# A two-layer attention backbone on one core: the row of maxima by one matmul and a copy, the modulation bias added at eviction, the last tiles' outputs in another order

## The chip, the core and the metric

The kernel runs on one core of a Trainium2 chip. Five engines work side by side, each through its own list of instructions in order: TensorE (PE, matmuls; PEld are its weight loads), VectorE (DVE), ScalarE (ACT), GpSimd (POOL) and SyncE (SP), which here issues nearly all DMAs. An engine whose next instruction waits holds up everything behind it in its list. Matmul results lie in PSUM banks and must be read out by DVE or ACT before a bank can be used again. The metric is the device time of one execution in microseconds, the median of three runs.

## The reference

Two layers over 1024 latent tokens and 256 context tokens of width 1024. Both layers modulate their input and gate their output by a vector made from the conditioning, `silu(c) @ w_mod + b_mod`; the first mixes by grouped-query attention, the second by neighbourhood attention, which leaves the context as it is.

```python
for i in range(DEPTH):
    mod_x = (silu_c @ w_mod[i] + b_mod[i])[:, None, :]
    mod_c = silu_cc @ w_mod[i] + b_mod[i]
    sh_x, sc_x, g_x = jnp.split(mod_x, 3, axis=-1)      # and sh_c, sc_c, g_c
    hx = rms_norm(x, norm_g[i]) * (1.0 + sc_x) + sh_x
    hc = rms_norm(ctx, norm_g[i]) * (1.0 + sc_c) + sh_c
    # layer 0: 16 query heads, 4 key/value heads, 1024 + 256 keys, softmax(q k^T / 8) v
    # layer 1: an 8 x 16 window plus the 256 context keys, with a learned bias
    # either branch: y = (o * silu(z)) @ w_out
    x = x + g_x * yx
return rms_norm(x, final_norm_g)
```

## The kernel before

Tokens go in ten tiles of 128 (eight latent, two context), and wide products in float16 pairs: a value is split into a rounded part and a remainder, and three matmuls stand for one. The eight *units* `u` of the first layer are pairs of query heads, with two heads `i` each; a unit has three *parts* `pt_`: latent tiles 0 to 3, 4 to 7, and the two context tiles.

**The row of maxima.** Head 0 of units 0 to 3, both heads of units 4 to 7, and both heads of every context part are computed with keys on the partitions. There the exponent's shift differs along the free dimension and cannot be a bias of the activation. So a first pass of matmuls (`pm`, `pmc`, in `mgen`) takes the maximum of the scores of every query (by DVE, into `mxp`), and the negated maxima are laid as an extra row, number 64, under the 64 rows of `q2`; the second score matmul (L1263, L1275) runs over 65 rows and adds it. The row is made in `rows` and `put_rows`: DVE reduces the maxima of a part's `n` tiles into `n` columns of a zeroed tile `zmax` (L1086). For tile `j` a matmul takes the 128 columns that begin at column `j`, so that the tile's maxima always come to stand in column 64 of what it loads, and its product with the identity puts them on partition 64 of `pr`. ACT then copies all `n` tiles, negated, on that one partition into row 64 of `q2` (L1111). There are 40 such groups: 24 with four tiles and 16 with two.

The second head of units 0 to 3 (`q_att`: tiles `qs`, `qpf`, `qpp`, `qpv`) is computed the other way, with queries on the partitions; its probabilities are transposed by DMA (L1207), and its row 64 is zero.

**The modulation.** `mod_block` makes, in blocks of 512 columns, what is needed beyond the first layer's shift and scale: eight blocks, spread over the eight units. Two halves of eight fp32 weight slices are loaded (`wg`), matmuls in 32-column tiles put the four quarters on the four groups of partitions, and one more group of four matmuls of depth one, `twos` by `brow` (L639), adds twice the bias, since all is halved afterwards. DVE copies the first half (L641), adds the second (L643), halves it, and with `r == 1` (scale) adds one and multiplies with the norm's weight. DMAs carry the rows to `gate_d` or `mod_d`.

**The end.** The output product of the second layer is taken in parts: `b_part(t, hf, range(K1))` sums six of the eight units for tile `t` and column half `hf` into `acc`, in PSUM banks with the tag "pj"; `b_out(t)` adds the last two units (banks "st"), squares and sums (ACT, `jk`, `fss`), takes the root (`ms_fin`, then a power on POOL, `rs_fin`), multiplies (ACT and POOL for one half, DVE for the other; for tile 7 DVE for both) and stores.

**What sets the order.** Pieces of work are generators with a begin and an end on a time line of units (`timeline`); this gives the order in which the instructions are written down. A `Planner` then runs through all instructions of the program: for each engine it takes the first ready one by rank, with assumed durations and landing times of DMAs; from the result it works out due times, which become the next ranks, five rounds long; the best order is fixed by dependencies. Hence a change at one place can move work elsewhere.

## Time and profile before

| | |
|---|---|
| Three runs | 1343.81, 1339.9, 1344.84 us (median 1343.81) |
| Profiled execution | 1343.95 us, span 1342.2 us |
| Mean granted clock of PE | 0.993 |
| PE busy | 1309.3 us, 98% of the span |
| DVE, ACT, POOL busy | 80%, 72%, 67% |
| First layer's attention | about 100 to 697 us |
| Matmuls of the row of maxima (L1110) | 128, 14.0 us busy with their drains |
| Bias matmuls (L639) | 64 instructions in 8 groups |
| PE's last matmul ends | 1331.25 us |

Rows of the timeline give start, duration, engine, source line, operation, output and inputs; several of a kind in a row are drawn together (`x4`). In brackets stands how long the engine was idle before, and whose end released it. A matmul's duration includes its drain, which overlaps the next matmul, so that the distance of two starts tells what a matmul costs in a stream.

### The profile page before, as it was taken

The numbers are of one execution on the slowest core, as the hardware profiler recorded it, in microseconds if no ns is written. First come the engines' busy times: TensorE is split into PE (matmuls) and PEld (weight loads), VectorE is DVE, ScalarE is ACT, GpSimd is POOL, SyncE is SP. The second block draws the span as 40 slices with busy tenths as digits, with TensorE's granted clock in tenths as the row PEclk, the third lists the DMA queues.
The fourth block names the chain that finished last, engine by engine and source line by source line (L and its number), as shares of the span: only waits on it lengthen the run. The fifth ranks groups of instructions, "written<-read, shape, count | busy, mean of one in ns | idle before, by whom it ended". The sixth has DMA issues, their size and how long they took to land.

```text
span 1342.2 us, 38615 instructions
## 1 busy us (share of the span) xinstructions
PE 1309.3 (98%) x15100; PEld 929.4 (69%) x15100; DVE 1075.4 (80%) x2456; ACT 971.2 (72%) x2076; POOL 895.4 (67%) x1214
## 2 busy tenths in 40 slices
PE   8999999999999999999999989999999999999996
PEld 4567777777777777776654448879687786967552
DVE  5898787879889786769528997889888898988465
ACT  4653989888889777698742456778888888887443
POOL 2323787777786767687875456687677878868443
PEclk9999999999999999999999999999999999999998
DMA  9824477687875422253418962679777878789952
GB/s 360 249 69 115 91 143 133 143 167 143 150 142 122 74 70 69 58 120 103 118 50 204 222 146 75 115 152 157 154 136 153 153 139 162 142 162 231 276 139 102
DMA packets 390497, 191.64 MB, mean 143 GB/s; under 512 B 349793, under 2 KB 355105, under 8 KB 390313
## 3 DMA queue, kind: packets, MB, share of 16 engines
q1 hardware_dynamic: 389736, 189.13, 63.7%
q8 instruction: 118, 1.93, 0.6%
q14 instruction: 67, 0.54, 0.1%
q10 hardware_dynamic: 576, 0.03, 0.0%
HBM read 91.03 MB, written 15.75 MB: 80 GB/s over the span
## 4 chain that ended last, share of the span: by engine, by line
PE 79%; DVE 10%; ACT 5%; issue 2%; DMA 2%; POOL 1%; DVEq 0%; POOLq 0%; SPq 0%; ACTq 0%
PE pa L1036 14%; PE poa L1360 7%; PE pob L1741 6%; PE st L1262 3%; PE st L1263 3%; PE pm L1070 3%; PE pv L1139 2%; PE pv L1140 2%; PE pv L1138 2%; PE pkv L889 2%; PE pbc L1529 1%; PE bpv L1650 1%; PE qs L1188 1%; PE qpv L1213 1%; DVE wb L1441 1%
## 5 line engine op out<-in xcount | busy, mean ns | idle before, releaser
L1132 POOL TENSOR_TENSOR pl<-pf,ph 128x256 f16<-128x256 f32 x400 | 276.8, 716 | 85.5 <-ACT pf L1249 65.0
L1132 POOL TENSOR_TENSOR bph<-bpf,bph 128x256 f16<-128x256 f32 (+1 forms) x224 | 185.6, 854 | 102.1 <-ACT bpf L1639 79.3
L1036 PE MATMUL pa<-wa,x 128*128 128x256 f16 x1536 | 222.5, 273 | 0.3 <-DVE mrow L641 0.3
L1247 ACT ACTIVATE ph<-st 128x512 f16<-128x512 f32 x240 | 143.3, 604 | 60.7 <-PE st L1263 56.2
L1567 PEld LDWEIGHTS <-hx 128*128 128x128 f16 x2688 | 157.6, 98 | 11.7 <-issue 3.8
L1036 PEld LDWEIGHTS <-x 128*128 128x128 f16 x1536 | 140.4, 98 | 33.1 <-issue 2.0
L1249 ACT ACTIVATE pf<-st 128x512 f32<-128x512 f32 x240 | 143.7, 607 | 1.6 <-DVE pl L1129 1.3
L1071 DVE TENSOR_REDUCE mxp<-pm 128x1 f32<-128x512 f32 x192 | 127.4, 685 | 12.0 <-PE pm L1070 9.8
L1138 PE MATMUL pv<-v,ph 128*128 128x65 f16 x960 | 124.0, 193 | 0.0
L1139 PE MATMUL pv<-v,ph 128*128 128x64 f16 x960 | 123.6, 195 | 0.0
L1140 PE MATMUL pv<-v,pl 128*128 128x65 f16 x960 | 122.5, 192 | 0.0
L1132 POOL TENSOR_TENSOR qpp<-qpf,qpp 128x256 f16<-128x256 f32 (+1 forms) x158 | 93.4, 613 | 33.5 <-ACT qpf L1205 23.4
L1519 PEld LDWEIGHTS <-wb 128*128 128x128 f16 x672 | 63.4, 98 | 70.6 <-issue 7.2
L1637 ACT ACTIVATE bph<-bpf,bnx 128x384 f16<-128x384 f32 (+1 forms) x128 | 70.4, 582 | 52.5 <-DVE bnx L1629 43.0
L1138 PEld LDWEIGHTS <-ph 128*128 128x128 f16 x960 | 91.0, 97 | 22.4 <-issue 0.4
L1139 PEld LDWEIGHTS <-ph 128*128 128x128 f16 x960 | 90.6, 97 | 16.6 <-issue 0.2
L1140 PEld LDWEIGHTS <-pl 128*128 128x128 f16 x960 | 91.1, 99 | 9.8 <-issue 0.8
L1262 PE MATMUL st<-q,k 128*128 128x512 f16 x240 | 90.9, 379 | 2.0 <-ACT pf L1249 1.1
L1263 PE MATMUL st<-q,k 65*128 65x512 f16 x240 | 91.0, 381 | 0.0
L1360 PE MATMUL poa<-woa,oa 128*128 128x512 f16 x384 | 89.4, 379 | 0.0
L1436 POOL TENSOR_TENSOR wtb<-wsb 128x256 f32<-128x256 f32 x64 | 59.5, 931 | 32.7 <-DMA wsb<-in_b_wp 22.1
L1741 PE MATMUL pob<-wob,obf 128*128 128x512 f16 x336 | 79.7, 379 | 0.6 <-DVE ms_fin L660 0.6
(485 smaller groups left out, 4063.2 us busy)
## 6 DMA issues: line engine op xcount, KB each, us to landing
wg<-in_w_mb SPq DMA_DIRECT2D x32, 512.0 KB
wsb<-in_b_wp SPq DMA_DIRECT2D x64, 256.0 KB
wm<-in_w_m SPq DMA_DIRECT2D x16, 512.0 KB
wsa<-in_a_wq SPq DMA_DIRECT2D x32, 256.0 KB
xstage<-in_x SPq DMA_DIRECT2D x8, 512.0 KB
wsoa<-in_a_w_out SPq DMA_DIRECT2D x16, 256.0 KB
x<-in_x SPq DMA_DIRECT2D x8, 512.0 KB
x_d<-x SPq DMA_DIRECT2D x8, 512.0 KB
```

Source lines behind the costliest of these rows:

```text
L1036: T.matmul(ps[:, :, i, :], hA(a, kt, t), wt[w][:, kt, :], start=n == 0, stop=n == 3 * KT - 1)
L1132: G.tensor_tensor(lo[:, c], p32[:, c], hi[:, c], op=ALU.subtract)
L1138: T.matmul(pv[:, t, :], hi[:, c], v[:, 0:65], start=first and t == 0, stop=False)
L1139: T.matmul(pv[:, t, 0:HD], hi[:, c], v[:, 65:129], start=False, stop=False)
L1140: T.matmul(pv[:, t, :], lo[:, c], v[:, 0:65], start=False, stop=last and t == n - 1)
L1247: S.activation(ph, st, AF.Exp)
L1249: S.activation(p32, st, AF.Exp)
L1262: T.matmul(so, k1[:, g, kc], q1[:, :, i, :], start=True, stop=False)
L1263: T.matmul(so, k2[0:65, g, kc], q2[0:65, :, i, :], start=False, stop=True)
L1360: T.matmul(ps, lhs(a, kt), w[b][:, kt, :], start=n == 0, stop=n == 3 * KT - 1)
L1567: T.matmul(ps[:, t * P:(t + 1) * P], hx[a][:, t, blk, kt], wt[j][:, s_, w, kt], start=first and t == 0 and m == 0, stop=last and t == 3 an ...
L1741: T.matmul(ps, ob[kt][:, t, a], wout["b"][hf][b][:, kt, :], start=n == 0, stop=n == 3 * len(kts) - 1)
```

## The change

It has three parts.

- `put_rows` makes one matmul a group: the maxima of the `n` tiles lie in columns 96 to 96+n of `zmax`, so the product with the identity has them on partitions 96 to 96+n. ACT copies these, negated, into rows 96.. of `q2`, which are otherwise unused, and a DMA on SP moves the `n` rows into row 64. `pr` is now 128 columns wide.
- `mod_block` loads the bias into `row` by a DMA that spreads it over the partitions (`spread`, which the norm's row uses as well), and both halves are added by one DVE operation, `ps * 0.5 + row`. The bias matmuls, `twos` and `brow` go, and with them a use of the staging buffers; the halving goes too.
- The first-pass parts of half 1 for tiles 4 to 7 get places late on the time line, each just ahead of the output of its tile.

```diff
--- before.py
+++ after.py
@@ -582,8 +582,6 @@
     scol = [main.tile([P, KT, 2], F32, name="scol")]
     gate_d = dram.tile([2, 2, D], F32, name="gate_d")
     mod_d = dram.tile([2, 2, D], F32, name="mod_d")
-    twos = main.tile([1, 32], F32, name="twos")
-    V.memset(twos, 2.0)
 
     def mod_cols(kt, pool):
 
@@ -620,35 +618,30 @@
         nm = f"{l}{c0}"
         r = c0 // D
         row = pool.tile([P, P], F32, name="mrow" + nm, tag="mrow", bufs=1)
+
+        def spread(dst, a):
+            DM.dma_start(dst, bass.AP(a.tensor, a.offset, [[P, 4], [0, 32], [1, P]]))
+
         for hf in range(2):
             wm = pool.tile([P, KT // 2, 512], F32, name=f"wg{nm}{hf}", tag="wg", bufs=1)
             for i in range(0, KT // 2, 2):
                 kt = hf * KT // 2 + i
                 DM.dma_start(wm[:, i:i + 2], w_mb[n, :, kt:kt + 2])
                 yield 2.0
-            if hf:
-                brow = com.tile([P, 512], F32, name="brow" + nm, tag="stage", bufs=4)[0:1]
-                DM.dma_start(brow, b_mod[l:l + 1, c0:c0 + 512])
+            if not hf:
+                spread(row, b_mod[l:l + 1, c0:c0 + 1])
             ps = ps_pj(f"pmg{nm}{hf}", shape=(P, 2, P))
             for i in range(KT // 2):
                 for j in range(4):
                     T.matmul(ps[32 * j:32 * j + 32, 0], s2[:, hf * KT // 2 + i, :], wm[:, i, j * P:(j + 1) * P],
-                             start=i == 0, stop=not hf and i == KT // 2 - 1)
-            if hf:
-                for j in range(4):
-                    T.matmul(ps[32 * j:32 * j + 32, 0], twos, brow[:, j * P:(j + 1) * P], start=False, stop=True)
-            if not hf:
-                V.tensor_copy(row, ps[:, 0])
-            else:
-                V.tensor_tensor(row, ps[:, 0], row, op=ALU.add)
+                             start=i == 0, stop=i == KT // 2 - 1)
+            V.scalar_tensor_tensor(row, ps[:, 0], 0.5, row, op0=ALU.mult, op1=ALU.add)
         if r == 1:
             gr = pool.tile([P, P], F32, name="gr" + nm, tag="gr", bufs=1)
-            g0 = ng_row[l:l + 1, c0 - D:c0 - D + 1]
-            DM.dma_start(gr, bass.AP(g0.tensor, g0.offset, [[P, 4], [0, 32], [1, P]]))
-            V.tensor_scalar(row, row, 0.5, 1.0, op0=ALU.mult, op1=ALU.add)
-            V.tensor_tensor(row, row, gr, op=ALU.mult)
-        else:
-            V.tensor_scalar_mul(row, row, 0.5 / WS if r == 2 else 0.5)
+            spread(gr, ng_row[l:l + 1, c0 - D:c0 - D + 1])
+            V.scalar_tensor_tensor(row, row, 1.0, gr, op0=ALU.add, op1=ALU.mult)
+        elif r == 2:
+            V.tensor_scalar_mul(row, row, 1.0 / WS)
         for v in range(2):
             dst = gate_d[l, v, c0 - 2 * D:c0 - 2 * D + 512] if r == 2 else mod_d[r, v, c0 % D:c0 % D + 512]
             DM.dma_start(dst.rearrange("(j c) -> j c", c=P), row[v:P:32])
@@ -999,7 +992,7 @@
     PT0, PTN = (0, 4, 8), (4, 4, 2)
     KCH = ((0, 512), (512, 512), (1024, 256))
     pairs = {}
-    zmax = [aq.tile([P, P + 4], F16, name=f"zmax{j}", bufs=1) for j in range(2)]
+    zmax = [aq.tile([P, P], F16, name=f"zmax{j}", bufs=1) for j in range(2)]
     for z in zmax:
         G.memset(z, 0.0)
     nrow = [0]
@@ -1083,8 +1076,8 @@
             for i in ((0,) if pt_ < 2 and u in QH else (0, 1)):
                 zm = zmax[nrow[0] % len(zmax)]
                 nrow[0] += 1
-                V.tensor_reduce(zm[:, 64:64 + n], mxs[i] if pt_ < 2 else mxs[i][:, 0:n, 2:3], axis=AX.X, op=ALU.max)
-                put_rows(zm, q2[64:65, :, i, :], n, f"{u}{pt_}{i}")
+                V.tensor_reduce(zm[:, 96:96 + n], mxs[i] if pt_ < 2 else mxs[i][:, 0:n, 2:3], axis=AX.X, op=ALU.max)
+                put_rows(zm, q2[:, :, i, :], n, f"{u}{pt_}{i}")
                 yield 200
 
         items = []
@@ -1105,10 +1098,10 @@
 
     def put_rows(zm, dst, n, nm):
 
-        pr = ps_mx(f"pr{nm}")
-        for j in range(n):
-            T.matmul(pr[:, j * P:(j + 1) * P], zm[:, j:j + P], id16, start=True, stop=True)
-        S.activation(dst, pr[64:65, 0:n * P].rearrange("p (t q) -> p t q", q=P), AF.Copy, bias=CSH, scale=-1.0)
+        pr = ps_mx(f"pr{nm}", shape=(P, P))
+        T.matmul(pr, zm, id16, start=True, stop=True)
+        S.activation(dst[96:96 + n, 0], pr[96:96 + n], AF.Copy, bias=CSH, scale=-1.0)
+        DM.dma_start(dst[64:65], dst[96:96 + n, 0])
 
     def o_evict(pool, pv, og, n, sz, t0, i, nm):
 
@@ -1764,10 +1757,10 @@
     items.append((once(b_open), 7.0, 7.01, 1))
     for hf in range(2):
         for t in range(NX):
-            v = 7.03 + 0.058 * (NX * hf + t)
+            v = 7.03 + 0.058 * (NX * hf + t) if not hf or t < 4 else 8.0 + 0.15 * (t - 4)
             items.append((b_part(t, hf, range(K1), "pj"), v, v + 0.058, 640 * K1))
     for t in range(NX):
-        v = (7.61 if t < 4 else 7.65) + 0.09 * t
+        v = 7.61 + 0.09 * t if t < 4 else 8.06 + 0.15 * (t - 4)
         items.append((b_out(t), v, v + 0.09, 2560))
     run_all(timeline(items))
```

Line numbers after are seven lower in the functions concerned (L1263 is L1256 then). In the lists below names end in a tile's number, which differs between the two programs.

On PE at the first row of maxima (unit 0, part 0); `pr` is the row matmul, `st` the score matmuls that use the row, `qs` those of the other head, which don't need it, `pm` the pass for the maxima of the next part, `pa` the next unit's projection. Before:

```order
L1110 MATMUL pr000_1531<-id16_71,zmax0_1242 128x128
...
L1070 MATMUL pm02000_1563<-k1_124,q101_1404 128x512
...
L1188 MATMUL qs0000_1605<-k1_124,q100_1253 128x512
...
L1263 MATMUL st0000_1592<-q200_1254,k2_125 128x512
...
L1263 MATMUL st0001_1654<-q200_1254,k2_125 128x512
...
L1189 MATMUL qs0000_1605<-k2_125,q200_1254 128x512
...
L1188 MATMUL qs0001_1631<-k1_124,q100_1253 128x512
...
L1189 MATMUL qs0001_1631<-k2_125,q200_1254 128x512
...
L1036 MATMUL pa10_1615<-wa10_1247,x00_103 128x2x128
```

and now:

```order
L1102 MATMUL pr000_1529<-id16_71,zmax0_1240 128x128
...
L1063 MATMUL pm02000_1559<-k1_122,q101_1402 128x512
...
L1181 MATMUL qs0000_1601<-k1_122,q100_1251 128x512
...
L1182 MATMUL qs0000_1601<-k2_123,q200_1252 128x512
...
L1181 MATMUL qs0001_1627<-k1_122,q100_1251 128x512
...
L1182 MATMUL qs0001_1627<-k2_123,q200_1252 128x512
...
L1063 MATMUL pm02001_1638<-k1_122,q101_1402 128x512
...
L1181 MATMUL qs0002_1663<-k1_122,q100_1251 128x256
...
L1182 MATMUL qs0002_1663<-k2_123,q200_1252 128x256
...
L1256 MATMUL st0000_1588<-q200_1252,k2_123 128x512
...
L1256 MATMUL st0001_1650<-q200_1252,k2_123 128x512
...
L1029 MATMUL pa10_1611<-wa10_1245,x00_101 128x2x128
```

The two `st` matmuls moved behind all `qs` matmuls of the tile and one more `pm`.

On SP in unit 7, where the row copies of part 0 stand among loads of output weights (`wsoa`, each into a staging buffer) and the copies of `q`. Before:

```order
L1058 DMA_TRANSPOSE q170_10893<-q1670_11167 128x8x128
L1148 DMA_TRANSPOSE oa6_11577<-oo60_11578 128x8x128
L1305 DMA wsoa01_12914<-in_a_w_out 128x512
L1059 DMA q270_10894<-q170_10893 64x1024
L1305 DMA wsoa11_12918<-in_a_w_out 128x512
L1305 DMA wsoa21_12952<-in_a_w_out 128x512
L1305 DMA wsoa31_12959<-in_a_w_out 128x512
L1058 DMA_TRANSPOSE q171_11476<-q1672_11757 128x8x128
L1305 DMA wsoa41_12984<-in_a_w_out 128x512
```

and now:

```order
L1051 DMA_TRANSPOSE q170_10822<-q1670_11092 128x8x128
L1141 DMA_TRANSPOSE oa6_11496<-oo60_11497 128x8x128
L1298 DMA wsoa31_12865<-in_a_w_out 128x512
L1052 DMA q270_10823<-q170_10822 64x1024
L1298 DMA wsoa41_12890<-in_a_w_out 128x512
L1104 DMA q270_10823<-q270_10823 1x4x128 x2
L1298 DMA wsoa51_12897<-in_a_w_out 128x512
L1051 DMA_TRANSPOSE q171_11395<-q1672_11676 128x8x128
L1298 DMA wsoa61_12952<-in_a_w_out 128x512
```

The two row copies (`q270`, one for each head) stand between two weight loads, and the transposes of the next part behind them.

On DVE at the end of the program; `acc<-pob` adds a product to a tile, `fss` adds the two halves' square sums, `ms_fin` makes the mean, and the multiplication by `fg` is the last step of a tile. In a name such as `pob510` the first digit is the tile, the second the half, the third the first unit summed. Before:

```order
L1753 TENSOR_TENSOR fss50_24801<-fss50_24801,fss51_24802 128x1
L1744 TENSOR_TENSOR acc_23682<-pob616_24845,acc_23682 128x512
L660 TENSOR_SCALAR ms_fin_24824<-fss50_24801 128x1
L1744 TENSOR_TENSOR acc7_23683<-pob706_24867,acc7_23683 128x512
L1753 TENSOR_TENSOR fss60_24833<-fss60_24833,fss61_24834 128x1
L660 TENSOR_SCALAR ms_fin_24856<-fss60_24833 128x1
L1758 SCALAR_TENSOR_TENSOR acc_23682<-acc_23682,rs_fin_24826,fg_23706 128x512
L1744 TENSOR_TENSOR acc7_23683<-pob716_24877,acc7_23683 128x512
L1758 SCALAR_TENSOR_TENSOR acc_23682<-acc_23682,rs_fin_24858,fg_23706 128x512
L1753 TENSOR_TENSOR fss70_24865<-fss70_24865,fss71_24866 128x1
L660 TENSOR_SCALAR ms_fin_24888<-fss70_24865 128x1
L1758 SCALAR_TENSOR_TENSOR acc7_23683<-acc7_23683,rs_fin_24890,fg_23706 128x512 x2
```

and now:

```order
L1737 TENSOR_TENSOR acc_23588<-pob610_24686,acc_23588 128x512
L1737 TENSOR_TENSOR acc_23588<-pob606_24721,acc_23588 128x512
L1737 TENSOR_TENSOR acc_23588<-pob616_24731,acc_23588 128x512
L1746 TENSOR_TENSOR fss60_24719<-fss60_24719,fss61_24720 128x1
L653 TENSOR_SCALAR ms_fin_24746<-fss60_24719 128x1
L1751 SCALAR_TENSOR_TENSOR acc_23588<-acc_23588,rs_fin_24748,fg_23612 128x512
L1737 TENSOR_TENSOR acc7_23589<-pob710_24738,acc7_23589 128x512
L1737 TENSOR_TENSOR acc7_23589<-pob706_24773,acc7_23589 128x512
L1737 TENSOR_TENSOR acc7_23589<-pob716_24783,acc7_23589 128x512
L1746 TENSOR_TENSOR fss70_24771<-fss70_24771,fss71_24772 128x1
L653 TENSOR_SCALAR ms_fin_24794<-fss70_24771 128x1
L1751 SCALAR_TENSOR_TENSOR acc7_23589<-acc7_23589,rs_fin_24796,fg_23612 128x512 x2
```

Before, the steps of tiles 5, 6 and 7 stand mixed; now one tile's steps end before the next one's additions begin, and each first-pass addition (`pob610`, `pob710`) stands between the tiles. Between the first layer's end and the last two units of the second PE's list is the same in both programs, numbers aside, and the other engines' lists very nearly so.

## Prediction

> **What bounds the kernel.** I read the page's busy shares first, then the busy time by stage, then what the tensor engine waits for, then the places of the three edits in the timeline. The page:
>
> ```profile
> span 1342.2 us, 38615 instructions
> PE 1309.3 (98%) x15100; PEld 929.4 (69%) x15100; DVE 1075.4 (80%) x2456; ACT 971.2 (72%) x2076; POOL 895.4 (67%) x1214
> ```
>
> Four stretches (columns: stretch and length; busy us of PE, weight loads, DVE, ACT, POOL; clock; DMA share; GB/s):
>
> ```profile
> 0.00:100.00 100.00, 94.89 (x611) 51.12 (x612) 80.71 (x209) 55.64 (x112) 27.60 (x37) 0.98 0.70 227
> 100.00:697.00 597.00, 590.06 (x7472) 442.40 (x7470) 462.85 (x1156) 474.81 (x1033) 438.83 (x643) 1.00 0.52 110
> 697.00:1239.00 542.00, 532.65 (x6364) 388.30 (x6362) 474.54 (x970) 396.09 (x831) 385.61 (x489) 1.00 0.77 156
> 1239.00:1342.20 103.20, 91.66 (x663) 47.58 (x660) 57.26 (x124) 44.67 (x101) 43.33 (x47) 0.96 0.66 178
> ```
>
> The first layer's attention, from about 100 to 697 us, holds the first two edits. PE is busy there for 590.06 of 597 us and no other engine passes 475, so PE sets the pace: work taken from PE shortens this stage by the same amount, unless a new wait fills it. The third edit lies in the last stretch, where PE stops about 11 us before the end.
>
> **Rows of maxima: what goes.** Each of 40 row groups (24 of four tiles, 16 of two) had one matmul a tile, 128 in all, and now has one: 88 go. In the timeline four of them take 0.22 us (618.03 to 618.25), 0.055 each; 0.39 is the drain of the last, which lies under the next matmul.
>
> ```profile
> 618.03 0.39 PE L1110 MATMUL pr<-id,zmax 128*128 128x128 f16 x4
> 618.25 0.27 PE L1036 MATMUL pa<-wa,xc_hi 128*128 128x256 f16 x1
> ```
>
> That is 88 x 0.055 = 4.8 us. Counted with the drain it would be 0.39 / 4, 8.6 us; the start of the next matmul says 0.055, so I take 4.8, and 8.6 as the far end; no row suggests less. The Trainium skill ("TensorE: Matmul & The Clock Gate", Back-to-back issue gap) gives about 81 ns per sustained 128-column matmul with its load, which would make this gain 7.1; the trace's 55 ns decides against it here.
>
> The ACT copy shrinks too. It took 358 ns at least for 256 elements and 588 for 512 in the median:
>
> ```profile
> L1111 ACT ACTIVATE q<-pr x40: 358/588/590, 124.1 to 655.1; 1x512 f16<-1x512 f32 x24, 1x256 f16<-1x256 f32 x16
> ```
>
> By that slope 128 elements on n partitions take about 0.24 us. The 10 us or so that ACT saves lie beside PE and count as nothing.
>
> **Rows: what comes.** Behind the copy stands a DMA from partitions 96.. to partition 64, 40 of them on SP's queue. The score matmul that adds the row (L1263, L1256 after) must now wait for its landing. No such DMA is in the trace. Its nearest relatives:
>
> ```profile
> 113.50 1.16 SPq L1059 DMA_DIRECT2D q<-q  x2
> ...
> 271.46 1.21 SPq L1207 DMA_TRANSPOSE qpp<-qpp  x1
> ...
> 275.56 0.23 PE L1213 MATMUL qpv<-v,qpp 128*128 128x128 f16 x1 [0.98 <-DMA qpp<-qpp]
> ```
> ```profile
> SPq L1059 <- DMA q<-q: 5.7, 5, 1.7
> ```
>
> An issue takes 0.58 us (half of 1.16). From the end of the issue to landing: SP itself, right behind a transpose's issue, waited 1.1 us (5.7 over 5) and at most 1.7, a lower end; PE got its transposed tile 2.9 us after an issue ended (272.67 to 275.56), the upper one. I take 2.0, between them, for a far smaller transfer of the same queue. So from row matmul to usable row: 0.22 (matmul) + 0.6 (ACT's lag, 123.45 to 124.09 below) + 0.24 + 0.05 + 0.58 + 1.1 to 2.9 = 2.8 to 4.6 us, 3.7 by my value. The Trainium skill ("DMA: Bandwidth & Descriptors", Anatomy of one DMA) puts a fixed 2.0 us on any DMA, issue and completion together, measured on another path; by it the chain would be 3.1 us and the term for late rows below nearly nothing, the second rival's time. No run here shows that yet.
>
> The place that is tight is the first row, unit 0 part 0:
>
> ```profile
> 123.23 0.38 PE L1110 MATMUL pr<-id,zmax 128*128 128x128 f16 x4 [0.62 <-DVE zmax L1086]
> ...
> 124.09 0.59 ACT L1111 ACTIVATE q<-pr 1x512 f16<-1x512 f32 x1
> ...
> 124.73 0.38 PE L1188 MATMUL qs<-k,q 128*128 128x512 f16 x1 [0.90 <-ACT q L1111]
> ...
> 124.95 0.59 PE L1263 MATMUL st<-q,k 65*128 65x512 f16 x2
> ...
> 126.11 0.68 DVE L1192 CUSTOM_DVE_ANT_0 qpf<-qs,zero 128x512 f32<-128x512 f32 x1
> ...
> 126.37 0.85 PE L1036 MATMUL pa<-wa,x 128*128 128x256 f16 x3
> ```
>
> ACT's copy at 124.09 now ends at 124.33, the issue at 124.96, and the row lands at 126.1 to 127.9. In the new order the qs matmuls that went behind the two st now go ahead of them; two PSUM banks and three DVE evictions of 0.68 (one of them of pm) with two 0.4 operations between hold these until about 127.1 anyway. So st starts near 127.2, and the first pa at 127.6 instead of 126.37: 1.2 late, less 0.4 of matmuls already done, 0.8 us (ends 0.2 and 1.5).
>
> For the other 39 I counted the PE work that the new order holds between a row's matmul and the first use of the row, at 0.055 us for 128 columns and 0.215 for 512 (three from 1329.80 to 1330.44, below), other widths scaled. Thirty-one have over 8 us, one 6.5. Seven have under 6: unit 1 part 0 5.9, unit 4 part 0 5.2, unit 2 part 0 4.9, unit 3 parts 0 and 1 4.3 and 4.2, unit 7 parts 0 and 1 4.1 and 3.6. Against 3.7 all but one are just in time, against 4.6 four are late by 0.3 to 1.0. Unit 7 part 1 meets a full queue, at 650.9 in the trace:
>
> ```profile
> 648.00:650.00 2.00, 2.00 (x26) 1.37 (x25) 2.00 (x4) 1.57 (x3) 1.02 (x3) 1.00 1.47 381
> 652.00:654.00 2.00, 2.00 (x34) 1.49 (x33) 1.17 (x3) 1.98 (x5) 1.17 (x2) 1.00 0.74 246
> ```
>
> The backlog ends near 653.5, a row then lands near 655.5, and its use stands at 650.9 + 3.6 = 654.5: 1.0 late. With some 1.0 for the other six together I put 2.0 us, ends 0 and 5. What else the new DMAs hold up: SP issues in order, and behind a row copy that waits for ACT stand the transposes of the second head's weights; PE waited for those 1.0 us in the whole run, and 40 more issues of 0.58 are 23 us of SP time in 597.
>
> **Bias.** Eight blocks lose four fp32 matmuls each (eight instructions), with a change of tile shape ahead of them:
>
> ```profile
> 190.76 0.15 PEld L639 LDWEIGHTS pmg<-brow,twos 1*32 1x32 f32 x8 [0.20 <-issue]
> 190.76 0.42 PE L639 MATMUL pmg<-brow,twos 1*32 1x128 f32 x8
> ...
> 191.11 0.10 PEld L1138 LDWEIGHTS <-phc 128*128 128x128 f16 x1 [0.20 <-DVE sz L1044]
> ```
>
> From 190.76 to 191.11 is 0.35 us, one load group and one gap of 0.20; the other gap stays, as a change of shape follows L635 in any case. 8 x 0.35 = 2.8 us (ends 1.2, the loads alone, and 5.0, matmuls and a gap). DVE's copy and add of a block become two scalar_tensor_tensor, and four blocks lose one operation: nothing on PE's path. The bias now comes by a 64 KB spread DMA per block, issued before the block's first matmul: hidden; at 110 GB/s for a share of 0.52 (second stretch) it is 0.3 us of the queue each, 2.5 for eight if the cover went.
>
> **The end.**
>
> ```profile
> 1303.36 2.10 PE L1741 MATMUL pob<-wob,obf 128*128 128x512 f16 x9
> 1305.30 0.60 PE L1152 MATMUL pob<-idf,bog 128*128 128x128 f32 x4
> ...
> 1320.63 0.81 PE L1741 MATMUL pob<-wob,ob 128*128 128x512 f16 x3
> ...
> 1321.07 0.16 DVE L1753 TENSOR_TENSOR fss<-fss,fss 128x1 f32<-128x1 f32 x1 [0.20 <-ACT jk L1752]
> ...
> 1321.47 0.69 DVE L1744 TENSOR_TENSOR acc<-pob,acc 128x512 f32<-128x512 f32 x1 [0.24 <-PE pob L1741]
> ...
> 1322.26 0.63 ACT L1752 ACTIVATE jk<-acc 128x512 f32<-128x512 f32 x1 [1.22 <-DVE ms_fin L660]
> ...
> 1329.80 0.81 PE L1741 MATMUL pob<-wob,obf 128*128 128x512 f16 x3 [0.59 <-DVE ms_fin L660]
> ...
> 1330.44 0.81 PE L1741 MATMUL pob<-wob,ob 128*128 128x512 f16 x3
> ...
> 1332.67 0.61 ACT L1752 ACTIVATE jk<-acc 128x512 f32<-128x512 f32 x1
> 1333.19 0.19 ACT L1752 ACTIVATION_READ_ACCUMULATOR jk<-acc 128x1 f32 x1
> 1333.75 1.21 DVE L1753 TENSOR_TENSOR fss<-fss,fss 128x1 f32<-128x1 f32 x1
> ...
> 1335.88 1.41 DVE L1758 SCALAR_TENSOR_TENSOR acc<-acc,rs_fin,fg 128x512 f32<-128x512 f32 x2 [0.73 <-POOL rs_fin L662]
> ```
>
> Before, four tiles finish 2.6 us apart and their normalisations pile up: PE loses 0.59 at 1329.80, and the last tile's square sum waits behind tile 6's work on ACT, its 0.16 us add takes 1.21 while POOL multiplies. From PE's end (1331.25) to the last product (1337.29) pass 6.0 us. In the new order 18 matmuls (3.9 us) stand between two tiles' outputs, and the last tile's operations have no other tile's behind PE. Undisturbed: 0.03 (1321.44 to 1321.47) + 0.69 + 0.10 + 0.71 (square and its readout) + 0.19 (add) + 0.92 (from the add's end, 1334.96, over mean and power to 1335.88) + 1.41 = 4.05 us. Gain 1.9 to 2.0, plus 0.6: 2.5 us (ends 1 and 3.5). The 72 moved matmuls had filled waits of the last attention; in the new order outputs of tiles 0 to 3 fill them, and 12 matmuls (2.6 us) stand between the last bpv and the last transposes (L1152), where 9 (the first row above) did without a wait. The output DMAs behind are the same.
>
> **The sum.** -4.8 - 2.8 - 2.5 + 0.8 + 2.0 = -7.3 us, against the profiled execution's 1343.95 (1.75 around its span): 1336.6. The median of the three runs is 0.14 lower; they spread over 4.9 us, so 0.5%, 6.7 us, is about what a measurement can tell from no change. Between 697 us and the last attention pair PE's new order is row for row the old one, so I expect nothing to be given back there.
>
> **Rivals.** *A second half-speed window* (0.10): at the first row PE's clock falls to 0.50:
>
> ```profile
> 126.00:127.00 1.00, 1.00 (x5) 0.55 (x4) 1.00 (x4) 1.00 (x3) 0.00 (x0) 0.50 0.03 8
> 129.00:130.00 1.00, 1.00 (x7) 0.52 (x5) 1.00 (x3) 0.30 (x1) 1.00 (x3) 0.96 0.60 207
> ```
>
> It lasted some 3.4 us, after PE had been half idle from 122.6 to 125. PE now idles there about 2 us longer; another such stretch costs 3.4 / 2 = 1.7: 1338.3. The Trainium skill ("TensorE: Matmul & The Clock Gate", Part 1) says the clock halves after an idle window of about 3.4 us and returns after a busy one; the trace agrees in length, and by that rule this rival is what longer idling does. *All rows in time* (0.15): only the first costs, 0.3, and the time is 1343.95 - 10.1 + 0.3 = 1334.2. *Rows late by SP's queue* (0.12): copies issue behind transposes waiting for POOL.
>
> ```profile
> SPq L1207 <- POOL qpp L1132: 40.1, 23, 4.4
> SPq L1305 <- DVE woa L733: 31.1, 9, 10.4
> ```
>
> At 1.7 us a wait (40.1 / 23) on the tight seven less what slack they have, some 5 us more: 1341.6, no change. *Slower* (0.08): unit 7's row copies stand on SP behind weight loads waiting for a staging buffer, as in the second row, up to 10.4 us; both parts held that long is 20.8 on PE, 1357. It decides once lateness passes the 14 us that separate 1336.6 from 1350.7.
>
> **Numbers.** The likeliest has 0.55, its own range 1333.5 to 1339.5, two thirds of it under 1337.1: 0.37 faster, 0.18 same. With the rivals: faster 0.37 + 0.15 = 0.52, same 0.18 + 0.10 + 0.12 = 0.40, slower 0.08. Range 1332 to 1343: the sum with rows free and the larger matmul price below, the late rows above.
>
> **What would show it.** Right: 40 row matmuls and no L639 group, PE busy 7 to 8 us less, PE waits on the q copy of 1 to 4 us in all, the largest at the first row and near 650, and about 4.1 us from PE's last matmul to the last product. Wrong: PE idle between 100 and 697 grown by over 10 us, or single waits on a row over 3 us.

## The result, and the profile after

| | before | after |
|---|---|---|
| Median of nine executions each | 1340.58 us (1338.76 to 1344.84) | 1336.4 us (1333.63 to 1337.45) |
| Ratio, with its 95% interval | | 0.9963 (0.9952 to 0.9975) |
| Profiled execution, and its span | 1343.95, 1342.2 us | 1334.24, 1332.5 us |
| PE busy, number of matmuls | 1309.3 us, 15100 | 1300.4 us, 14948 |

The change is 4.2 us faster by the medians and 5.0 us by the ratio (3.4 to 6.4): a real gain, but under the 0.5%, 6.7 us, that the prediction put as the bound of "same", so that of its two likelier outcomes (faster 0.52, same 0.40) the second came. The forecast time, 1336.6, was met. How it was met is another matter: two of its terms were off by 1.4 and 4.9 us, in opposite directions, and its base lay 3.4 us too high.

The base first. The sum was made against a profiled execution of 1343.95 us. Nine executions have their median at 1340.58, so that one lay 3.4 us above it, while the profiled execution of the changed kernel was 2.2 us under its median. The two traces therefore differ by 9.7 us where the kernels differ by 4 to 5, and a stretch can't be read from their difference alone. Below, the trace of the kernel with the tail part alone (run e3) stands in for "before" in the first layer: up to the last stretch its lists are those of before, and its profiled execution lies on its median.

The page of the changed kernel, and its time by the same stages as before (length; busy us of PE, weight loads, DVE, ACT, POOL; clock; DMA share; GB/s):

```profile
span 1332.5 us, 38402 instructions
...
PE 1300.4 (98%) x14948; PEld 923.5 (69%) x14948; DVE 1071.4 (80%) x2451; ACT 966.0 (72%) x2076; POOL 888.1 (67%) x1214
```
```profile
100.00:697.00 597.00, 586.59 (x7334) 438.86 (x7332) 460.30 (x1155) 469.77 (x1035) 436.97 (x645) 0.99 0.53 112
697.00:1239.00 542.00, 533.21 (x6396) 389.55 (x6395) 478.10 (x979) 397.71 (x834) 383.73 (x491) 1.00 0.77 159
1239.00:1332.50 93.50, 85.99 (x610) 44.37 (x608) 52.10 (x111) 42.44 (x96) 39.85 (x42) 0.98 0.66 175
```

PE is busy 8.9 us less than in the trace of before and 6.9 us less than in e3's (1307.3); the forecast was 7 to 8. In the first layer it now idles 10.4 of 597 us, where before it was 6.9: part of what was taken away came back as waits. What PE waited for there (total, times, longest):

```profile
PE qpv L1206 <- DMA qpp<-qpp: 2.9, 3, 2.1
PE qs L1181 <- DVE qmx L1185: 1.5, 3, 0.6
PE st L1255 <- ACT pf L1242: 1.3, 2, 1.0
```

No wait on a row copy is in this list: in the order that the planner chose, no row came too late to be seen. The largest wait is on transposed weights of the other head, at one place. The timeline there, and the stretches around it (the granted clock is the third column from the end):

```profile
278.55 0.19 PE L1131 MATMUL pv<-v,ph 128*128 128x65 f16 x1
280.88 0.29 PE L1206 MATMUL qpv<-v,qpp 128*128 128x128 f16 x1 [2.14 <-DMA qpp<-qpp]
```
```profile
280.00:281.00 1.00, 0.12 (x2) 0.13 (x3) 0.00 (x0) 0.35 (x1) 1.00 (x2) 0.92 0.53 113
281.00:282.00 1.00, 1.00 (x17) 1.00 (x17) 0.00 (x0) 0.26 (x1) 0.11 (x1) 0.50 1.29 274
...
284.00:285.00 1.00, 1.00 (x10) 0.81 (x9) 0.69 (x3) 0.00 (x0) 0.54 (x1) 0.87 0.00 0
```

PE stands for 2.1 us, and then runs at half clock for some 3.4 us, from about 280.8 to 284.3: 2.1 + 1.7 = 3.8 us lost at one place. The kernel with the row part alone (run p1 below) has both at the same place: a wait of 2.16 us at 279.60 and half clock from about 280.7 on. No row copy is among SP's issues from 262 to 281 in either, so it is no late row that PE waits for here; what makes this transpose late in the new order stays open. The half clock is the prediction's second half-speed window, at a place where it was not looked for. The first row of maxima, where it was looked for:

```profile
123.72 0.22 PE L1102 MATMUL pr<-id,zmax 128*128 128x128 f16 x1 [0.62 <-DVE zmax L1079]
...
124.58 0.27 ACT L1103 ACTIVATE q<-pr 4x128 f16<-4x128 f32 x1
...
124.88 0.69 SPq L1104 DMA_DIRECT2D q<-q  x1
124.90 0.38 PE L1181 MATMUL qs<-k,q 128*128 128x512 f16 x1 [0.75 <-ACT q L1103]
...
126.29 0.38 PE L1063 MATMUL pm<-k,q 128*128 128x512 f16 x1 [0.35 <-DVE qmx L1185]
...
127.23 0.37 PE L1181 MATMUL qs<-k,q 128*128 128x256 f16 x1 [0.57 <-DVE qmx L1185]
...
127.61 1.06 PE L1256 MATMUL st<-q,k 65*128 65x512 f16 x2
```

The `st` matmuls begin at 127.61 (forecast 127.2). And the end of the program, which answers to the last block of the prediction:

```profile
1324.18 0.81 PE L1734 MATMUL pob<-wob,ob 128*128 128x512 f16 x3
...
1325.03 0.69 DVE L1737 TENSOR_TENSOR acc<-pob,acc 128x512 f32<-128x512 f32 x1 [0.60 <-PE pob L1734]
...
1326.84 0.16 DVE L1746 TENSOR_TENSOR fss<-fss,fss 128x1 f32<-128x1 f32 x1 [1.12 <-ACT jk L1745]
...
1327.92 1.41 DVE L1751 SCALAR_TENSOR_TENSOR acc<-acc,rs_fin,fg 128x512 f32<-128x512 f32 x2 [0.73 <-POOL rs_fin L655]
```

From PE's last matmul (1324.99) to the last product (1329.33) pass 4.34 us, against 6.04 before and 4.05 forecast; the square sum's add takes 0.16 again. From the last product to the end pass 3.17 us, where before it was 4.91 (1337.29 to 1342.2). SP's issues of the output DMAs tell why; before, and after:

```profile
1336.65 1.80 SPq L1762 DMA_DIRECT2D out<-acc  x4
```
```profile
1328.70 1.00 SPq L1755 DMA_DIRECT2D out<-acc  x2
```

Before, the last four stores were issued one behind another from 1336.65 on, and the last issue ended at 1338.45, 1.16 us after the last product; now only two are left by then, and the last issue ends at 1329.70, 0.37 after the product. From there to the end pass 3.75 us before and 2.80 now, presumably because fewer stores are still on their way.

### The profile page after: what moved, and what is told of

The parts are those of the page before. It is cut to its first block, busy times and chain, and to the rows that moved or that the text cites. A ratio compares the mean times of both kernels' runs of the same rounds, so it can differ in the third digit from the quotient of the medians.

```text
span 1332.5 us, 38402 instructions
## 1 busy us (share of the span) xinstructions
PE 1300.4 (98%) x14948; PEld 923.5 (69%) x14948; DVE 1071.4 (80%) x2451; ACT 966.0 (72%) x2076; POOL 888.1 (67%) x1214
## 4 chain that ended last, share of the span: by engine, by line
PE 74%; DVE 12%; ACT 6%; DMA 4%; issue 2%; POOL 1%; SPq 0%; DVEq 0%; POOLq 0%; ACTq 0%
PE pa L1029 13%; PE poa L1353 7%; PE pob L1734 6%; PE st L1256 3%; PE st L1255 3%; PE pm L1063 3%; PE pv L1132 2%; PE pv L1133 2%; PE pv L1131 2%; DVE wb L1434 1%; PE pkv L882 1%; DMA qpp<-qpp 1%; PE pbc L1522 1%; PE qpv L1206 1%; PE qs L1181 1%
## 5 line engine op out<-in xcount | busy, mean ns | idle before, releaser
L1125 POOL TENSOR_TENSOR pl<-pf,ph 128x256 f16<-128x256 f32 x400 | 271.7, 703 | 67.8 <-ACT pf L1242 44.0
L1029 PE MATMUL pa<-wa,x 128*128 128x256 f16 x1536 | 226.0, 273 | 0.5 <-DVE mrow L638 0.4
L1064 DVE TENSOR_REDUCE mxp<-pm 128x1 f32<-128x512 f32 x192 | 127.3, 685 | 16.3 <-PE pm L1063 14.2
L1256 PE MATMUL st<-q,k 65*128 65x512 f16 x240 | 91.2, 383 | 0.0
```

The costliest lines, as they stand in the source:

```text
L1029: T.matmul(ps[:, :, i, :], hA(a, kt, t), wt[w][:, kt, :], start=n == 0, stop=n == 3 * KT - 1)
L1125: G.tensor_tensor(lo[:, c], p32[:, c], hi[:, c], op=ALU.subtract)
L1256: T.matmul(so, k2[0:65, g, kc], q2[0:65, :, i, :], start=False, stop=True)
```

## The experiments

Each run was timed in five rounds against the kernel before on the same chip. In the table a difference is (ratio - 1) x 1340; the intervals reach 1.1 to 1.9 us to either side.

| run | what | median us | ratio (95%) | difference us |
|---|---|---|---|---|
| e1_rows | rows alone | 1339.6 | 0.9990 (0.9982 to 0.9999) | -1.3 |
| e2_bias | bias alone | 1345.9 | 1.0038 (1.0024 to 1.0052) | +5.1 |
| e3_tail | tail alone | 1336.36 | 0.9971 (0.9960 to 0.9981) | -3.9 |
| e4_nocopy | rows without the row copy | 1343.82 | 1.0024 (1.0011 to 1.0036) | +3.2 |
| p1_rows | rows, fourth round of plan | 1339.42 | 0.9985 (0.9974 to 0.9996) | -2.0 |
| p2_bias | bias, fourth round | 1342.27 | 1.0016 (1.0005 to 1.0026) | +2.1 |
| p3_nocopy | rows without copy, fourth round | 1342.88 | 1.0022 (1.0012 to 1.0033) | +2.9 |
| p4_round2 | before, second round | 1343.48 | 1.0022 (1.0012 to 1.0031) | +2.9 |
| f1_bias_fixed | bias, order of before | 1344.27 | 1.0028 (1.0017 to 1.0040) | +3.8 |
| f2_rows_fixed | rows, order of before | 1342.1 | 1.0012 (1.0000 to 1.0025) | +1.6 |
| f4_tail_bias | tail and bias, order of tail alone | 1341.46 | 1.0011 (1.0000 to 1.0021) | +1.5 |
| f5_two_rows | the same, bias buffers in turn | 1338.35 | 0.9991 (0.9979 to 1.0003) | -1.2 |

### The three parts alone

Each kernel is the one before with its hunks of the diff and nothing else: e1 with those of `zmax`, `rows` and `put_rows`, e2 with those of `twos` and `mod_block`, e3 with the one of the time line.

> The kernel before with the row part of the change alone. Theory A (the prediction's terms): 88 matmuls less, -4.8 us; first row late, +0.8; other rows late, +2.0: 2.0 us faster than before. Theory B (the traces of before and after: the first pv came 2.2 us late, not 0.8, and PE waited 1.9 us longer for transposed weights behind the row copies on SP): -4.8 + 2.2 + 1.9 + some 1 for other waits, 0.3 us slower to 0.7 us faster. Theory C (the copies cost little and the missing gain is in the bias part): 4 us faster.

> The kernel before with the bias part alone. Theory A: eight groups of matmuls at 0.35 us go: 2.8 us faster. Theory B (the order around the blocks is planned anew, and what is won there is filled with other waits): within 1 us of before. Theory C (the spread DMA is late and PE or DVE waits for it): slower than before, with a wait on the mrow DMA in the list of waits.

> The kernel before with the tail part alone. Theory A: 2.5 us faster, of which 1.9 to 2.0 from PE's last matmul to the last product (6.0 us before, 4.1 now) and 0.6 in PE's list; the stores behind the last product as before (4.9 us to the end). Theory B (the profile after: the stores ended 1.7 us sooner too, since fewer stores lie behind one another): 4.2 us faster, with 3.2 us from the last product to the end. Theory C (the profiled execution of before was a slow one at its end too): 1 us or less faster.

The tail alone is worth as much as the whole change: 3.9 us by the ratio, 4.3 by the medians. Its trace has the two gains of the changed kernel's end: 4.07 us from PE's last matmul (1327.03) to the last product (1331.10, below), and 3.5 from there to the end of its span (1334.6). So Theory B holds for it, the stores included.

```profile
1326.22 0.81 PE L1741 MATMUL pob<-wob,ob 128*128 128x512 f16 x3
...
1329.68 1.42 DVE L1758 SCALAR_TENSOR_TENSOR acc<-acc,rs_fin,fg 128x512 f32<-128x512 f32 x2 [0.73 <-POOL rs_fin L662]
```

The rows alone gain 1.3 us. The bias part, forecast at -2.8, costs 5.1. In both of these the traces showed a loss where neither part is at work: from the first matmul of the last output product to the last `bpv` they take 76.45 and 76.47 us, where the kernel with the tail part takes 73.61 and the kernel before 73.56. The planner keeps the round of plan whose own forecast is shortest; before, after and tail alone it is the fourth, here it was the second, and with it the whole second layer stands in another order.

### What the round of plan is worth

The p kernels keep the same round as the kernel before:

```diff
-            best = min(best, (self.schedule(key.__getitem__, margin=margin), self.order), key=lambda b: b[0])
+            best = (self.schedule(key.__getitem__, margin=margin), self.order)
...
-        plan.refine(5, 100.0, 200.0)
+        plan.refine(4, 100.0, 200.0)
```

In p4 nothing else is changed, and the number is 2.

> The kernel before, nothing changed but the planner's second round kept in place of its fourth. Theory A (the other round is what the single parts lost in the last stretch): 2 to 4 us slower than before, with 76 us from the first output matmul to the last bpv in place of 73.6. Theory B (the round does not matter): within 1 us of before.

> The row part alone, the planner's fourth round kept as in the kernel before (of itself it took its second round here, and with it another order through the whole second layer). Theory A (the row part is worth what its first layer showed, and the other round of plan hid it): PE reached the end of the first layer's attention 2.0 us earlier than in the kernel with the tail part alone, whose first layer is that of before, and the last stretch lost 2.9: so 2 to 3.5 us faster than before. Theory B (the round does not matter): 1.0 us faster, as without the fixed round.

> The bias part alone, the planner's fourth round kept. Theory A (the prediction's term): 2.8 us faster than before. Theory B (the other round cost 2.9 us in the last stretch, and the rest, some 2 us, was lost in the first layer's attention whatever the round): 2 us slower. Theory C (the round does not matter): 5 us slower, as without the fixed round.

The other round alone costs 2.9 us (p4). Its last stretch, from the first of these rows to the end of the last, against the same rows of the kernel with the tail part (second fence), takes 75.36 us in place of 73.61:

```profile
1228.11 0.82 PE L1741 MATMUL pob<-wob,obf 128*128 128x512 f16 x3 [1.40 <-DMA obf<-ob_d]
...
1303.28 0.19 PE L1651 MATMUL bpv<-bv,bpht 128*128 128x65 f16 x1
```
```profile
1226.44 0.82 PE L1741 MATMUL pob<-wob,obf 128*128 128x512 f16 x3
...
1299.86 0.19 PE L1651 MATMUL bpv<-bv,bpht 128*128 128x65 f16 x1
```

That is 1.8 of the 2.9 us, in a stretch for which the theory gave 76 and 73.6; where the rest goes these rows don't show. With the round fixed, rows are worth -2.0, bias +2.1 and tail -3.9: together -3.8, inside the interval of the whole change (-6.4 to -3.4). So the parts about add up with the round held. For the bias part the round made 3.0 us; for the rows 0.7, within the intervals, so that p1 doesn't tell its theories apart. Theory B of p2 holds in its size: some 2 us are lost whatever the round. What PE waits for in p2's first layer is another thing than in the runs with the old order below: no wait on a transposed tile of 0.2 us or more is in its list, and what grew are waits on ACT and DVE:

```profile
PE qs L1181 <- ACT q L1104: 1.8, 3, 0.9
PE pmg L636 <- DVE q L817: 1.5, 1, 1.5
```

In e3 these two are 0.9 and 0.3 us. What brings them in p2 was not tested.

### The row without its copy

ACT writes a row in one copy again, and no DMA follows.

```diff
-        S.activation(dst[96:96 + n, 0], pr[96:96 + n], AF.Copy, bias=CSH, scale=-1.0)
-        DM.dma_start(dst[64:65], dst[96:96 + n, 0])
+        S.activation(dst[64:65], pr[64:65].rearrange("p (t q) -> p t q", t=1).broadcast_to([1, n, P]), AF.Copy, bias=CSH, scale=-1.0)
...
-            S.activation(ph, st, AF.Exp)
+            S.activation(ph, st, AF.Exp, scale=0.02)
```

> The row part alone, without the row copy on SP: ACT writes the maxima of a part's first tile into the row of all its tiles with one copy of 512 (or 256) elements on one partition, as long as the copy of before. The maxima of the other tiles are left out, and the first layer's exponentials of this route have a scale of 0.02, so that they stay finite. Theory A: the 88 matmuls are gone and no row is late: 4.8 us faster than before, 2.8 faster than the row part alone. Theory B: also 4.8 us faster than before, and 4 to 5 us faster than the row part alone. Theory C (the matmuls were under other work and their going is worth less): less than 2.5 us faster than before.

> The row part without the row copy on SP, as in the earlier run (the maxima of all tiles but a part's first left out, a scale of 0.02 in the exponentials), the planner's fourth round kept. Theory A (late rows cost the prediction's 2.8 us): 4.8 us faster than before and 2.8 faster than the row part with the copy. Theory B (the copies cost next to nothing; what is won on PE is lost to waits that a new order brings): within 1 us of the row part with the copy.

Both were slower than the row part with its copy, by 4.5 and 4.9 us, which no theory had. The profiled executions don't tell why: they are the fastest of their runs (1341.32 and 1338.43 us, the medians 1343.82 and 1342.88), and the second is in its trace even ahead of p1. The order differs too, since the planner counts the longer ACT copy and no DMA. Nor does the clock: at the same mean granted clock, 0.995, e4 took 1343.1 us on average (four executions) and e1 1339.6 (seven). These two runs say nothing on what the copy costs, and the next one was made for that.

### The order held still

A new kernel has a new order, and that alone moved the time by 3 us. So in the f kernels the planner plans the kernel before, and the changed program gets that order instruction by instruction: what is gone is left out, what replaces an operation stands in its place, and only the new DMAs need a place of their own.

```diff
+        order = {e: [to[m] for m in o if m in to] for e, o in old.order.items()}
+        for k in fresh:
...
+            if "mrow" in b[k][2]:
+                w = [m for m in o if m < k and m in back]
+                prev = {m for m in w if "mrow" in b[m][-1] or b[m][2] == b[k][2].replace("mrow", "wg") + "0"}
+                o.insert(max(map(o.index, prev)) + 1, k)
+            else:
+                t = max(old.done[back[m]] for m in self.pred[k] if m in back and self.eng[m] == "ACT")
+                n = next((n for n, m in enumerate(o) if m in back and old.start[back[m]] >= t), len(o))
+                o.insert(n, k)
```

> The row part alone, in the order of the kernel before: three of four (one of two) row matmuls a group taken out, the row copy put on SP where the planned end of ACT's copy falls, nothing else moved. In this order the first use of a row stands nearer to its matmul than in the changed kernel: five rows have under 3.7 us of PE work between (0.7, 1.8, 2.7, 3.3 and 3.6 us). Theory A (a row needs 3.7 us from its matmul): the late rows cost 6.4 us and the matmuls give 4.8: 1.6 us slower than before, and PE's list of waits shows about 6 us on the row copies, 3 of them at the first row. Theory B (a row needs 2.8 us or less, or the copies collide with nothing): 3.2 us or less for late rows, so 1.6 us faster or more. Theory C (SP held up by the copies): the transposes come late too, and it is 5 us slower or more.

Here the rows are late, and PE's list of waits in the first layer says by how much:

```profile
PE st L1328 <- DMA q<-q: 4.2, 4, 1.4
PE pmg L693 <- DMA wg<-in_w_mb: 2.6, 2, 1.8
```

At the first row the chain reads:

```profile
122.74 0.22 PE L1169 MATMUL pr<-id,zmax 128*128 128x128 f16 x1 [0.62 <-DVE zmax L1145]
...
123.60 0.27 ACT L1170 ACTIVATE q<-pr 4x128 f16<-4x128 f32 x1
...
123.93 0.71 SPq L1171 DMA_DIRECT2D q<-q  x1
...
125.68 0.59 PE L1328 MATMUL st<-q,k 65*128 65x512 f16 x2 [1.39 <-DMA q<-q]
```

From the row's matmul to its first use pass 2.94 us; at the second and third of the four waits 4.06, where ACT came late, and 2.78. The copy is usable 1.04 us after its issue ends (124.64 to 125.68), at the other two 1.77 and 1.08. The waits on rows, 4.2 us, lie between Theory A (6.4) and Theory B (at most 3.2). With the 4.8 gained and the second row, 1.8 us more than in e3, they make +1.2, and +1.6 was measured. But the trace has a loss more. Behind the two waits for `wg`, at 627.63 and 629.10, the clock is halved for some 6.8 us, and that is 3.4 us:

```profile
631.00:633.00 2.00, 2.00 (x16) 1.12 (x15) 1.23 (x3) 1.09 (x2) 0.54 (x1) 0.50 0.85 188
```

Of f2's twelve executions the seven with a mean clock of 0.994 or less took 1341.85 to 1346.46 us, the five above it 1338.15 to 1341.3. So the +1.6 (0.0 to 3.4) is in part half clock that comes in some executions, and the sum checks the terms only roughly. What the matmuls give can be read directly, since the order is the same: around one group of four, in e3 and in f2:

```profile
464.86 0.39 PE L1110 MATMUL pr<-id,zmax 128*128 128x128 f16 x4
465.08 0.27 PE L1036 MATMUL pa<-wa,xc_hi 128*128 128x256 f16 x1
```
```profile
464.86 0.22 PE L1169 MATMUL pr<-id,zmax 128*128 128x128 f16 x1
464.92 0.27 PE L1094 MATMUL pa<-wa,xc_hi 128*128 128x256 f16 x1
```

The next matmul comes 0.16 us sooner for three that are gone, about 0.055 each, as forecast. So a row copy isn't free where its row is wanted at once; the changed kernel shows none because its order puts other matmuls ahead of `st`.

> The bias part alone, in the order of the kernel before: its planned order is kept instruction by instruction on every engine, only the bias matmuls and their loads are taken out, DVE's operations replaced where they stood, and the spread DMA put behind the loads of its block's first half. Theory A (the term was right, and a new order of the first layer ate it): 2.8 us faster than before, 4 to 5 us faster than the bias part in an order of its own. Theory B (the spread DMA or the two longer DVE operations are what costs): 1 us faster or less, or slower, with a wait on mrow in PE's, DVE's or SP's lists.

> Tail and bias part without the row part, in the order that the planner gives the kernel with the tail part alone. Theory A (the terms add when the order stays): 4.3 + 2.8 = 7.1 us faster than before, 1333.4, and faster than the changed kernel by 3 us. Theory B (the bias part is worth nothing in this order either): 4.3 us faster, as the tail part alone.

In an order that is the old one row for row, the bias part costs 3.8 us (f1), and 5.4 us on top of the tail part (f4 against e3). So the loss needs no new order: the edit costs by itself. What goes was priced rightly. In f4 the next matmul comes 1.01 us after the first of a second half's 32, where it was 1.36 in e3 and before:

```profile
187.93 1.08 PE L698 MATMUL pmg<-wg,s 128*32 128x128 f32 x32
188.94 0.20 PE L1210 MATMUL pv<-v,phc 128*128 128x65 f16 x1
```

That is 0.35 us a block, 2.8 in all, so that what comes costs some 8 us in this order. What PE waited for in the first layer in f4, and then SP:

```profile
PE qpv L1285 <- DMA qpp<-qpp: 5.0, 5, 1.4
...
PE pmc L1148 <- DMA q<-q: 1.8, 1, 1.8
```
```profile
SPq L691 <- DMA mod_d<-mrow: 12.3, 4, 4.8
SPq L691 <- DMA gate_d<-mrow: 6.2, 3, 2.8
```

The spread DMA (L691) writes the bias into `row`, of which there is one buffer. The block before has its sums in that buffer, and they leave it by DMAs on the same queue. So SP issues these and then stands until they have ended, 18.5 us at the seven spreads that have a block before them, with everything behind it in its list. One such place; the rows are SP's issues:

```profile
389.71 1.12 SPq L726 DMA_DIRECT2D mod_d<-mrow  x2
394.56 0.58 SPq L691 DMA_DIRECT2D mrow<-in_b_mod  x1
395.26 3.94 SPq L1279 DMA_TRANSPOSE qpp<-qpp  x3
```

From 390.83 to 394.56 SP does nothing, three transposes of `qpp` come behind it, and PE's 6.8 us of waits on tiles that come through SP (0.2 in the kernel with the tail part alone) fit such lateness. The Trainium skill ("DMA: Bandwidth & Descriptors", Anatomy of one DMA) says that the DMA engines wait for no semaphore, and that such a wait takes place on the sequencer that issues the DMA; these rows agree. Before the change the bias went into one of four staging buffers. SP waited for these too (e3: 7.7 us in two waits of L631, on DVE's use of a staging buffer), and PE's transposed tiles were not late for it.

The last run takes this wait away by another buffer:

```diff
-        row = pool.tile([P, P], F32, name="mrow" + nm, tag="mrow", bufs=1)
+        tags = ("gr", "mrow") if NEW.get("bias") and n % 2 else ("mrow", "gr")
+        row = pool.tile([P, P], F32, name="mrow" + nm, tag=tags[0], bufs=1)
...
-            gr = pool.tile([P, P], F32, name="gr" + nm, tag="gr", bufs=1)
+            gr = pool.tile([P, P], F32, name="gr" + nm, tag=tags[1], bufs=1)
```

> Tail and bias part in the same order as in the run before it of these two parts (1341.46 us; there SP stood 18.5 us before its spread DMAs, until the DMAs that empty mrow had ended, and PE waited 6.8 us for transposes behind them), with one thing changed: blocks take turns between the two buffers mrow and gr, so that the spread DMA writes a buffer that was emptied a block earlier. The norm's row takes the other buffer and is loaded where the spread is. Theory A (SP's wait for mrow is what the bias part costs): SP's waits of 18.5 us go, PE's waits on transposed tiles fall from 6.8 us to 1.5 or less, and it is 7 us faster than before, 1333.5, below the changed kernel. Theory B (the 64 KB spread itself, many short packets ahead of the transposes on the same queue, is what costs): PE's waits on transposes stay at 4 us or more, and it is within 2 us of the run before it, 1339.5 or more.

```profile
PE qpv L1289 <- DMA qpp<-qpp: 2.9, 4, 1.2
...
PE pmc L1152 <- DMA q<-q: 0.7, 1, 0.7
```
```profile
SPq L717 <- DMA mod_d<-mrow: 5.2, 2, 2.9
```

The order is that of f4 but for the two loads of the norm's row. SP's waits before the spread are gone, PE's waits on SP's tiles fall from 6.8 to 3.6 us, and the kernel is 2.7 us faster than f4 by the ratios (about 0.6 to 4.8 with both intervals), 3.1 by the medians. So the wait for the buffer is shown to cost something, by these numbers about half of the 5.4 us that the bias part costs in this order. It is not all, and Theory A's 7 us didn't come. The norm's row, which I put into the other buffer, now waits there itself (5.2 us, L717): from 388.36 to 391.34 SP stands ahead of it, three transposes come behind, and 1.5 of PE's 3.6 us lie between 390 and 420. By ratio f5 is still 2.7 us behind the tail part alone, with PE busy 3.0 us less (1304.3 against 1307.3). How much of that rest is this new wait, and how much the spread's own packets ahead of the transposes, stays open.

No kernel of these beats the changed one; the tail part alone equals it within the intervals. The rows and the tail together, without the bias part, weren't run.

## Why the prediction was right, and where it was not

- **Rows, what goes (-4.8).** The matmuls went, and 0.055 us for each holds: 0.16 us for three, between the same neighbours in f2 and e3. The far end of 8.6 is out.
- **First row late (+0.8; ends 0.2 and 1.5).** Held. Between the row's matmul and the late `st` PE idles 0.75 + 0.35 + 0.57 = 1.67 us in the changed kernel, where before it idled 0.90 at this place: 0.8 us more. (In p1 5.03 us pass from the row's matmul to the first `pv`, in the same part without a copy, p3, 3.57; but more matmuls lie between in p1.) The copy was quicker than I took it; the score matmuls of the other head, DVE's evictions between them and one more `pm` are what holds `st` (it starts at 127.61, while by f2's 1.04 to 1.77 us from the end of the issue, 125.57, the row was there at 126.6 to 127.3).
- **Other rows late (+2.0).** Wrong in its place, and if it was right in its size that was chance. In the new order no row is a named wait, and unit 7, where I put 1.0, shows nothing. From the start of the copy's issue to the use f2 shows 1.72, 1.75 and 2.42 us, where I took 2.58. The Trainium skill's fixed 2.0 us for a DMA ("DMA: Bandwidth & Descriptors", Anatomy of one DMA), measured there on another path, was nearer. In their place stands the 2.1 us wait on `qpp` near 280 with a half-clock window behind it, in the changed kernel and in p1. The row part as a whole, forecast at -2.0, measured -2.0 (p1; interval -3.5 to -0.5).
- **Bias (-2.8).** The step that failed: "The bias now comes by a 64 KB spread DMA per block, issued before the block's first matmul: hidden". I priced the bytes (0.3 us of the queue each) and not the wait: the DMA must find `row` empty, and what empties it stands just ahead of it in the same queue. What goes was right, 0.35 us a block. In all it measured +3.8 in the old order (f1), in good part through SP's wait and the transposes behind it (f4 and f5), and +2.1 in the planner's own order (p2), where PE's list shows no late transposes and the cause stays open. In the changed kernel, whose planner chose the spreads' places, SP stands for them 5.6 us in place of 18.5 (below).

```profile
SPq L623 <- DMA mod_d<-mrow: 3.1, 4, 1.4
...
SPq L623 <- DMA gate_d<-mrow: 2.5, 1, 2.5
```

- **The end (-2.5).** Right in its mechanism, too small: -3.9 alone. The chain gave 2.0 in e3 and 1.7 in the changed kernel (forecast 1.9 to 2.0) and PE's list 0.75 (0.6: 26.98 us from the last `bpv` to the last matmul in place of 27.73). The step that failed is "The output DMAs behind are the same": four stores queued behind one another before, two now, and the end comes 1.7 us sooner after the last product.
- **The base.** -7.3 from 1343.95 gave 1336.6; from the median of nine before, 1340.58, it would have given 1333.3, under all nine executions after. The terms promised some 2 to 3 us too much, and the high base covered it.
- **Rivals.** The second half-speed window came, at 280.8 and not at the first row; it lasted 3.4 us again, which is the price of 1.7. All rows in time: true by PE's list, without the gain that I tied to it. Rows held behind SP's queue, and the slower case in unit 7, didn't show.

So the sum's terms -4.8 + 0.8 + 2.0 - 2.8 - 2.5 = -7.3 were measured as -2.0 for the rows, +2.1 for the bias and -3.9 for the end, and the changed kernel is 4 to 5 us faster because of its last part.

## What to carry to other kernels

A load moved into a buffer that a DMA of the same queue has just to leave isn't hidden by being early: look up what its buffer waits for, and then what stands behind it in that queue. Where a planner orders the program, no part of a change can be measured alone until the order is held: here a change of the planner's round, with no code behind it, cost 2.9 us, more than two of the three parts are worth. And when the last chain of a kernel is shortened, count the stores behind it too, as a queue of its own.

## What the runs showed that was not expected

- **The clock fell after a wait of 2.1 us.** In the changed kernel PE was busy until 278.74, idle to 280.88, and at half clock for the next 3.4 us; in p1 the clock fell near the same place after a wait of 2.16 us. The Trainium skill ("TensorE: Matmul & The Clock Gate", Part 1) puts an idle window of about 3.4 us ahead of that. Here 2.14 us were enough. At the first row the traces of before and after show such a window and that of the tail part alone, whose order is that of before, doesn't: it comes in some executions and not in others, which is 1.7 us of their spread.
- **A copy of four rows of 128 from partitions 96.. to partition 64** takes SP 0.62 us to issue in the median and is usable 1.04 to 1.77 us later.
- **Rows without their copy were slower** by 4.5 to 4.9 us than rows with it. The cause wasn't found.
